# The adaLN sums of a diffusion trunk step: folding half of each accumulator into the other half in place, and summing the remaining rows with products of ones

## The chip, the core and the metric

The kernel runs on one core of a Trainium2 chip. The core has a tensor engine (TensorE, PE in the profile; its weight loads are the line PEld), a vector engine (VectorE, DVE), a scalar engine (ScalarE, ACT), GpSimd (POOL), a queue engine that starts most transfers (SyncE, SP) and sixteen DMA engines. The metric is the device time of one execution in microseconds (us); the median of three runs is used.

## The reference, cut to what matters

One step of a trunk of two layers. Each layer is feed-forward, mixer, feed-forward, and each of these three is modulated by a shift, a scale and a gate. These nine vectors come from the conditioning: silu(c) for the 256 latent tokens and silu(c_ctx) for the 128 context tokens, times a matrix of 1024 x 9216 per layer, plus a bias.

```python
def part(i):
    return mod[:, i][:, None, :]            # mod = silu(c) @ w_ada + b_ada, nine parts of 1024

h = rmsnorm(x, p['g_ff1']) * (1 + part(1)) + part(0)
x = x + 0.5 * part(2) * swiglu(h, p['w1_gate'], p['w1_up'], p['w1_down'])
h = rmsnorm(x, p['g_mix']) * (1 + part(4)) + part(3)
y, ctx_state = mixer(h)
x = x + part(5) * y
h = rmsnorm(x, p['g_ff2']) * (1 + part(7)) + part(6)
x = x + 0.5 * part(8) * swiglu(h, p['w2_gate'], p['w2_up'], p['w2_down'])
```

Everything is in float32. The kernel computes each large product as three products of rounded parts (high x high, high x low, low x high).

## The kernel before, in words

**Large products.** The state is held transposed, 1024 features on partitions in 8 tiles, 384 tokens along the row. The functions `ffn` and `mixer` load weights in chunks of 128 x 1024 on the SP queue (L234), split each chunk into a rounded part `hi` (ScalarE, L243) and a rest `lo` (VectorE, L244), and multiply: `prod3` issues three matmuls of a 128x128 weight tile with 384 columns (L248 to L250). Four buffers of `hi` and four of `lo` hold the chunks, so the vector engine is at most two pairs of chunks ahead of TensorE. The tiles `pg` and `pu` are the gate and up products, `pd` the down product; L568 multiplies silu(gate) by up into `sg`.

**The conditioning product.** For a product with only two columns (the context and the latent stream) the kernel does not use TensorE, except for the first 16 feature tiles of layer 0. It is made beside the feed-forwards as a filler. A unit is up to three tiles of 128 output features (`units`): `ada_steps` loads 128 x 8 x 384 numbers of `w_ada` into one of two `flat` buffers (L264), and then in eight steps `ada_product` (L276 for the first step, L278 for the other seven) accumulates on VectorE, for each stream s, the eight row blocks times the conditioning value of each partition into `acc[:, s, :]` (tile `adacc`, 128 partitions x 2 streams x 384, two buffers that the units use in turn). What then remains is to sum each column of `acc` over its 128 partitions. There are 43 units: 42 of three tiles and one of two.

**The sum over partitions before.** `ada_reduce` (L295) does it in two stages. In the first, two transfers on the GpSimd queue (L298, L299) copy the lower half of stream 0 and the upper half of stream 1 crosswise into the tile `adfold`, and GpSimd adds the other halves to them (L302, one addition for each stream). The tile then holds 64 partial sums of stream 0 on the upper partitions and 64 of stream 1 on the lower ones, 384 columns. In the second stage TensorE transposes its three 128x128 tiles (L308) into a PSUM tile, ScalarE sums each half row of it with an accumulating activation (L310, six per unit), and VectorE adds the bias and multiplies by the gain (`ada_finish`, L268 and L269), which gives the tile `mod`.

**What sets the order.** The class `Filler` paces the units: the loops of `ffn` call it with a fixed number of steps for each chunk. When a unit's eighth step is done its first stage is issued, and the second is kept in the list `late` with a count of six steps; `flush` counts it down with each further step and then issues the second stage, marked to be placed after the latest product step (`tc.issue_after`). The mixer calls `flush(99)` (L766), which issues all that is left. A scheduler places all instructions on the five in-order queues by the order of issue and its own costs. The places that the prediction speaks of are the TensorE queue around L308, the vector queue around L276 and L268, and the GpSimd queue around L298 to L302. A row sum of another kind also counts: `rms_sum` (L416) sums a 128x384 tile over its partitions as three matmuls of 128x128 weights with a single column of ones; and L907 and L1081, in the mixer, are matmuls that contract over only 64 partitions.

Of the kernel before, what the change touches and what calls it, by code (L numbers as in the profile page):

```python
# [9 lines left out]
F32 = mybir.dt.float32  # L10
# [3 lines left out]
AF = mybir.ActivationFunctionType  # L14
ALU = mybir.AluOpType
AX = mybir.AxisListType

P = 128
# [72 lines left out]
def trunk_kernel(ctx: ExitStack, tc: tile.TileContext, I: dict, C: dict, O: list):  # L91
    nc = tc.nc
    V, S, G, T = nc.vector, nc.scalar, nc.gpsimd, nc.tensor
# [7 lines left out]
    sm = ctx.enter_context(tc.tile_pool(name="sm", bufs=2))  # L101
# [7 lines left out]
    def small(name):  # L109
        return psm.tile([P, 512], F32, tag="sm", name=name)  # L110
# [4 lines left out]
    def cload(name, shape, src, pool=None, eng=None):  # L115
        t = (pool or const).tile(shape, F32, name=name)
        (eng or nc.gpsimd).dma_start(out=t, in_=src)
        return t
# [46 lines left out]
    ident = cload("ident", [P, P], C["ident"], eng=nc.scalar)  # L165
    cols_b0 = columns("b0", [("b_ada0", row128(I["b_ada"][0:1]), 72, nc.scalar), ("g_ff1", row128(I["g_ff1"]), 16, nc.scalar)])
    ones = const.tile([P, P], F32, name="ones")
# [90 lines left out]
    junk = const.tile([P, P], F32, name="junk")  # L258
# [7 lines left out]
    def ada_finish(l, kt, n, sums):  # L266
        mp = mod[:, l, kt:kt + n, :]
        V.tensor_tensor(out=mp, in0=sums.rearrange("p (k s) -> p k s", s=2), in1=bc(badd[:, l, kt:kt + n].unsqueeze(2), [P, n, 2]), op=ALU.add)  # L268
        V.tensor_tensor(out=mp, in0=mp, in1=bc(bmul[:, l, kt:kt + n].unsqueeze(2), [P, n, 2]), op=ALU.mult)  # L269
# [24 lines left out]

    def ada_reduce(acc, l, kt, n):  # L295
        c = n * P
        fold = sm.tile([P, 3 * P], F32, tag="adfold", bufs=1, name="adfold")
        nc.gpsimd.dma_start(out=fold[0:64, :c], in_=acc[64:128, 0, :c])  # L298
        nc.gpsimd.dma_start(out=fold[64:128, :c], in_=acc[0:64, 1, :c])  # L299
        for s in range(2):  # L300
            h = slice(64 * s, 64 * s + 64)
            G.tensor_tensor(out=fold[h, :c], in0=acc[h, s, :c], in1=fold[h, :c], op=ALU.add)  # L302

        yield False
        pm = sm.tile([P, 6], F32, tag="adasum", bufs=2, name="adasum")
        pt = small(f"ada{l}_{kt}")
        for m in range(n):
            T.transpose(pt[:, m * P:(m + 1) * P], fold[:, m * P:(m + 1) * P], ident)  # L308
        for m in range(2 * n):
            S.activation(out=junk[:, 0:64], in_=pt[:, m * 64:(m + 1) * 64], func=AF.Identity, accum_out=pm[:, m:m + 1])  # L310
        ada_finish(l, kt, n, pm[:, :2 * n])

    def ada_steps(l, kt, n, stage):

        w = stage(n)
        ada_load(w, l, kt, n)
        yield True
        acc = ada_acc()
        for k in range(KD):
            ada_product(acc, w, n, k)  # L320
            if k < KD - 1:
                yield True
        red = ada_reduce(acc, l, kt, n)
        next(red)
        yield red
# [12 lines left out]
    class Filler:  # L338
# [24 lines left out]
        def flush(self, steps):  # L363
            for t in list(self.late):
                t[0] -= steps
                if t[0] < 0:
                    self.late.remove(t)
                    with tc.issue_after(last_step[0].ins):
                        next(t[1], None)

        def begin(self):
            for _ in range(2):
# [1301 lines left out]
```

## Time and profile before

| | |
|---|---|
| median of three runs | 1611.67 us (1611.38 to 1614.06) |
| profiled execution | 1614.9 us, span of its instructions 1613.1 us |
| granted TensorE clock, mean | 0.991 of full speed |
| TensorE | 97% of the span busy |
| VectorE | 77% |
| ScalarE | 49% |
| GpSimd | 16% |

The profile is of one execution. Times are in us from the start of the span. A row of a timeline gives the start, the time covered, the engine, the line of the kernel, the operation and its tiles (output <- input), and a count when several alike follow each other. A matmul of float32 operands that isn't one of the `prod3` kind stands twice in the trace, as two passes; a transpose stands once. Matmuls overlap, so what an insertion costs is read from the starts of the matmuls around it and not from the durations.

### The profile page before, as it was taken

The numbers are of one execution on the slowest core, as the hardware profiler recorded it, in microseconds if no ns is written. First come the engines' busy times: TensorE is split into PE (matmuls) and PEld (weight loads), VectorE is DVE, ScalarE is ACT, GpSimd is POOL, SyncE is SP. The second block draws the span as 40 slices with busy tenths as digits, with TensorE's granted clock in tenths as the row PEclk, the third lists the DMA queues.
The fourth block names the chain that finished last, engine by engine and source line by source line (L and its number), as shares of the span: only waits on it lengthen the run. The fifth ranks groups of instructions, "written<-read, shape, count | busy, mean of one in ns | idle before, by whom it ended". The sixth has DMA issues, their size and how long they took to land. (4 is left out here: it accounts for less than half of the span.)

```text
span 1613.1 us, 24761 instructions
## 1 busy us (share of the span) xinstructions
PE 1561.6 (97%) x9027; PEld 1467.4 (91%) x9027; DVE 1245.8 (77%) x2485; ACT 786.8 (49%) x1838; POOL 255.4 (16%) x334
## 2 busy tenths in 40 slices
PE   7899999999999999999999999999999999999997
PEld 5789989997867999999999999999886799999997
DVE  5799997997878699996999977698787767434333
ACT  5544434548465554444546344454846656333332
POOL 2112221232040001131220212123004000000000
PEclk9999999999999999999999999999999999999999
DMA  9757758664432367867676865675344234444341
GB/s 309 247 151 232 225 185 247 208 199 120 121 75 75 109 204 232 253 179 222 212 206 192 250 195 164 213 231 158 116 111 86 66 110 126 122 126 131 118 137 46
DMA packets 233375, 270.68 MB, mean 168 GB/s; under 512 B 12392, under 2 KB 217936, under 8 KB 233253
## 3 DMA queue, kind: packets, MB, share of 16 engines
q1 hardware_dynamic: 223232, 248.67, 50.8%
q0 software_dynamic: 9744, 20.31, 5.3%
q8 instruction: 71, 1.16, 0.3%
q14 instruction: 52, 0.42, 0.1%
q10 hardware_dynamic: 276, 0.11, 0.0%
HBM read 257.10 MB, written 3.57 MB: 162 GB/s over the span
## 5 line engine op out<-in xcount | busy, mean ns | idle before, releaser
L278 DVE SCALAR_TENSOR_TENSOR adacc<-flat,sc,adacc 128x384 f32<-128x384 f32 (+1 forms) x602 | 357.2, 646 | 0.0
L302 POOL TENSOR_TENSOR adfold<-adacc,adfold 64x384 f32<-64x384 f32 (+1 forms) x86 | 118.0, 1372 | 174.7 <-DMA adfold<-adacc 172.3
L253 ACT CAST ah<-sg 128x384 fp32r<-128x384 f32 x88 | 45.1, 513 | 163.1 <-DVE sg L568 162.3
L250 PE MATMUL pd<-ah,lo_db 128*128 128x384 f32 x352 | 118.8, 338 | 1.6 <-DVE lo_db L244 1.4
L250 PE MATMUL pd<-ah,lo_da 128*128 128x384 f32 x352 | 118.7, 337 | 1.6 <-DVE lo_da L244 1.6
L249 PE MATMUL pg<-wide,hi_gb 128*128 128x384 f32 (+1 forms) x352 | 119.3, 339 | 0.2
L248 PE MATMUL pd<-ah,hi_da 128*128 128x384 f32 x352 | 119.3, 339 | 0.0
L248 PE MATMUL pg<-wide,hi_gb 128*128 128x384 f32 (+1 forms) x352 | 119.2, 339 | 0.0
L248 PE MATMUL pd<-ah,hi_db 128*128 128x384 f32 x352 | 118.9, 338 | 0.0
L250 PE MATMUL pg<-wide,lo_gb 128*128 128x384 f32 (+1 forms) x352 | 118.5, 337 | 0.0
L249 PE MATMUL pu<-wide,hi_ub 128*128 128x384 f32 (+1 forms) x352 | 118.4, 336 | 0.0
L249 PE MATMUL pd<-al,hi_db 128*128 128x384 f32 x352 | 118.4, 336 | 0.0
L249 PE MATMUL pd<-al,hi_da 128*128 128x384 f32 x352 | 118.4, 336 | 0.0
L248 PE MATMUL pu<-wide,hi_ub 128*128 128x384 f32 (+1 forms) x352 | 118.2, 337 | 0.0
L250 PE MATMUL pu<-wide,lo_ub 128*128 128x384 f32 (+1 forms) x352 | 117.8, 337 | 0.0
L248 PE MATMUL pu<-wide,hi_ua 128*128 128x384 f32 (+1 forms) x328 | 111.3, 340 | 4.2 <-DVE sg L568 4.2
L250 PE MATMUL pg<-wide,lo_ga 128*128 128x384 f32 (+1 forms) x328 | 112.0, 343 | 1.9 <-DVE lo_ga L244 1.9
L248 PE MATMUL pg<-wide,hi_ga 128*128 128x384 f32 (+1 forms) x328 | 113.5, 346 | 0.0
L249 PE MATMUL pg<-wide,hi_ga 128*128 128x384 f32 (+1 forms) x328 | 112.0, 342 | 0.0
L298 POOL DMA_DIRECT2D adfold<-adacc x43 | 23.9, 556 | 550.5 <-DVE adacc L278 352.0
L249 PE MATMUL pu<-wide,hi_ua 128*128 128x384 f32 (+1 forms) x328 | 110.9, 338 | 0.0
L250 PE MATMUL pu<-wide,lo_ua 128*128 128x384 f32 (+1 forms) x328 | 110.6, 338 | 0.0
(504 smaller groups left out, 4290.9 us busy)
## 6 DMA issues: line engine op xcount, KB each, us to landing
flat<-in_w_ada_dram SPq DMA_DIRECT2D x42, 1536.0 KB, 8.1
st_gb<-in_w_gate_dram SPq DMA_DIRECT2D x44, 512.0 KB, 3.8
st_ub<-in_w_up_dram SPq DMA_DIRECT2D x44, 512.0 KB, 4.5
st_ga<-in_w_gate_dram SPq DMA_DIRECT2D x41, 512.0 KB, 3.9
st_ua<-in_w_up_dram SPq DMA_DIRECT2D x41, 512.0 KB, 4.9
st_da<-in_w_down_dram SPq DMA_DIRECT2D x40, 512.0 KB, 4.8
st_db<-in_w_down_dram SPq DMA_DIRECT2D x40, 512.0 KB, 3.5
wst<-in_w_ada_dram SPq DMA_DIRECT2D x8, 1024.0 KB, 12.6
```

The lines of the kernel that those rows point to most:

```text
L248: T.matmul(out, lhsT=lh, rhs=rh, start=start, stop=False)
L249: T.matmul(out, lhsT=lh, rhs=rl, start=False, stop=False)
L250: T.matmul(out, lhsT=ll, rhs=rh, start=False, stop=stop)
L253: S.copy(hi, src)
L278: last_step[0] = V.scalar_tensor_tensor(out=acc[:, s, :n * P], in0=w[:, k, :], scalar=sc[:, k, s:s + 1], in1=acc[:, s, :n * P], op0=ALU.mu ...
L298: nc.gpsimd.dma_start(out=fold[0:64, :c], in_=acc[64:128, 0, :c])
L302: G.tensor_tensor(out=fold[h, :c], in0=acc[h, s, :c], in1=fold[h, :c], op=ALU.add)
```

## The change

The copies crosswise and the GpSimd additions become two transfers that add into the accumulator itself: the lower half of stream 0 is added to its upper half, and the upper half of stream 1 to its lower half. The tile `adfold` and its additions go. In the second stage the transposes and the six accumulating activations go; instead, for each stream, up to three matmuls take 64 partitions x 128 columns of the accumulator as the stationary operand and a 64x1 column of ones as the moving one, and give the 128 sums of a tile directly as a column of PSUM; ScalarE copies three such columns at a time. The generator now yields its own delays (2 steps between the matmuls and `ada_finish`), and `flush` goes on with a unit as long as its delay is over.

```diff
     def ada_reduce(acc, l, kt, n):
         c = n * P
-        fold = sm.tile([P, 3 * P], F32, tag="adfold", bufs=1, name="adfold")
-        nc.gpsimd.dma_start(out=fold[0:64, :c], in_=acc[64:128, 0, :c])
-        nc.gpsimd.dma_start(out=fold[64:128, :c], in_=acc[0:64, 1, :c])
+        nc.gpsimd.dma_start(out=acc[0:64, 0, :c], in_=acc[64:128, 0, :c], accum_op=ALU.add)
+        nc.gpsimd.dma_start(out=acc[64:128, 1, :c], in_=acc[0:64, 1, :c], accum_op=ALU.add)
+
+        yield 2
+        pm = sm.tile([P, 6], F32, tag="adasum", bufs=2, name="adasum")
         for s in range(2):
             h = slice(64 * s, 64 * s + 64)
-            G.tensor_tensor(out=fold[h, :c], in0=acc[h, s, :c], in1=fold[h, :c], op=ALU.add)
-
-        yield False
-        pm = sm.tile([P, 6], F32, tag="adasum", bufs=2, name="adasum")
-        pt = small(f"ada{l}_{kt}")
-        for m in range(n):
-            T.transpose(pt[:, m * P:(m + 1) * P], fold[:, m * P:(m + 1) * P], ident)
-        for m in range(2 * n):
-            S.activation(out=junk[:, 0:64], in_=pt[:, m * 64:(m + 1) * 64], func=AF.Identity, accum_out=pm[:, m:m + 1])
+            pt = small(f"ada{l}_{kt}")
+            for m in range(n):
+                T.matmul(pt[:, m:m + 1], lhsT=acc[h, s, m * P:(m + 1) * P], rhs=ones[h, 0:1], start=True, stop=True)
+            S.copy(pm[:, s:2 * n:2], pt[:, :n])
+        yield 2
         ada_finish(l, kt, n, pm[:, :2 * n])
...
         def flush(self, steps):
             for t in list(self.late):
                 t[0] -= steps
-                if t[0] < 0:
-                    self.late.remove(t)
+                while t in self.late and t[0] < 0:
                     with tc.issue_after(last_step[0].ins):
-                        next(t[1], None)
+                        more = next(t[1], None)
+                    if more is None:
+                        self.late.remove(t)
+                    else:
+                        t[0] += more
```

On TensorE, at the unit whose sums are the tile `ada0_31` (layer 0, feature tiles 31 to 33), between the products of two weight chunks, the order before is:

```order
L249 MATMUL pu1_1875<-wide3_229,hi_ua07_0_1884 128x384
L250 MATMUL pu1_1875<-wide2_228,lo_ua07_0_1885 128x384
L308 MATMUL ada0_31_1988<-ident_92,adfold_1907 128x128 [waits PE_49,Pool_49]
L308 MATMUL ada0_31_1988<-ident_92,adfold_1907 128x128 x2
L248 MATMUL pg0_1872<-wide2_228,hi_ga07_4_1969 128x384
L249 MATMUL pg0_1872<-wide3_229,hi_ga07_4_1969 128x384
```

and in the changed kernel (L306 is its line of the products with ones):

```order
L249 MATMUL pu1_1860<-wide3_229,hi_ua07_0_1869 128x384
L250 MATMUL pu1_1860<-wide2_228,lo_ua07_0_1870 128x384
L306 MATMUL ada0_31_1970<-ones_97,adacc_1728 128x1 [waits DMASW4_49,PE_49]
L306 MATMUL ada0_31_1970<-ones_97,adacc_1728 128x1 x2
L306 MATMUL ada0_31_1975<-ones_97,adacc_1728 128x1 [waits DMASW5_49,PE_49]
L306 MATMUL ada0_31_1975<-ones_97,adacc_1728 128x1 x2
L248 MATMUL pg0_1857<-wide2_228,hi_ga07_4_1951 128x384
L249 MATMUL pg0_1857<-wide3_229,hi_ga07_4_1951 128x384
```

The place is the same; six products stand where three transposes stood, and they wait for the two transfers where the transposes waited for GpSimd.

On VectorE, where the accumulator of a new unit is first written (L276) while the sums of an earlier one are finished (L268, L269), the order before is:

```order
L568 TENSOR_TENSOR sg_1488<-sg_1488,pu1_1314 128x384 [waits PE_49,Activation_49]
L244 TENSOR_TENSOR lo_ua05_4_1603<-st_ua05_4_1600,hi_ua05_4_1602 128x1024 [waits DMAHW3_49,Activation_49]
L254 TENSOR_TENSOR al9_670<-sg_1488,ah9_669 128x384 [waits Activation_49]
L276 TENSOR_SCALAR adacc_1608<-flat1_1417,sc_99 128x384 [waits DMASW5_49,DMAHW4_49,DMASW4_49,Pool_49]
L276 TENSOR_SCALAR adacc_1608<-flat1_1417,sc_99 128x384
L278 SCALAR_TENSOR_TENSOR adacc_1608<-flat1_1417,sc_99,adacc_1608 128x384 [waits DVE_49] x2
L268 TENSOR_TENSOR mod_104<-adasum_1524,badd_101 128x6 [waits Activation_49]
```

and in the changed kernel:

```order
L254 TENSOR_TENSOR al9_670<-sg_1479,ah9_669 128x384 [waits Activation_49]
L244 TENSOR_TENSOR lo_ua05_4_1591<-st_ua05_4_1588,hi_ua05_4_1590 128x1024 [waits DMAHW3_49]
L268 TENSOR_TENSOR mod_104<-adasum_1515,badd_101 128x6 [waits Activation_49]
L276 TENSOR_SCALAR adacc_1596<-flat1_1408,sc_99 128x384 [waits DMASW5_49,DMAHW4_49,DMASW4_49,PE_49]
L269 TENSOR_TENSOR mod_104<-mod_104,bmul_102 128x6 [waits DVE_49]
L276 TENSOR_SCALAR adacc_1596<-flat1_1408,sc_99 128x384
L278 SCALAR_TENSOR_TENSOR adacc_1596<-flat1_1408,sc_99,adacc_1596 128x384 [waits DVE_49] x10
```

The first write of a reused accumulator waited for GpSimd's additions and now waits for TensorE, which reads the accumulator itself.

## Rows read from the trace of the kernel before

**Rows 1.** The page: busy time of each engine, share of the span, instructions

```profile
PE 1561.6 (97%) x9027; PEld 1467.4 (91%) x9027; DVE 1245.8 (77%) x2485; ACT 786.8 (49%) x1838; POOL 255.4 (16%) x334
```

**Rows 2.** Busy time by stretch: start:end, length, each engine, clock, DMA

```profile
200.00:300.00 100.00, 96.58 (x561) 95.67 (x561) 89.51 (x144) 41.47 (x108) 23.92 (x24) 1.00 0.71 221
...
1400.00:1500.00 100.00, 100.00 (x579) 100.00 (x578) 42.19 (x49) 36.11 (x48) 0.00 (x0) 1.00 0.44 127
```

**Rows 3.** Timeline of TensorE around the transposes of a unit

```profile
1010.76 0.34 PE L250 MATMUL pu<-wide,lo_ua 128*128 128x384 f32 x1
1010.94 0.49 PE L308 MATMUL ada<-ident,adfold 128*128 128x128 f32 x3
...
1011.44 0.34 PE L249 MATMUL pg<-wide,hi_ga 128*128 128x384 f32 x1
```

**Rows 4.** Line 308: all its transposes, duration min/median/max in ns

```profile
L308 PE MATMUL ada<-ident,adfold x128: 271/272/330, 114.5 to 1144.6; 128*128 128x128 f32 x128
```

**Rows 5.** Timeline of TensorE around a row sum over 128 partitions

```profile
563.61 0.34 PE L250 MATMUL pu<-wide,lo_ub 128*128 128x386 f32 x1
563.78 0.73 PE L416 MATMUL stb<-ones,accb 128*128 128x1 f32 x6
...
564.63 0.34 PE L249 MATMUL pg<-wide,hi_gb 128*128 128x386 f32 x1
```

**Rows 6.** Timeline of TensorE: four products over 64 partitions, in two blocks

```profile
395.86 0.71 PE L907 MATMUL pP<-qk 64*128 64x128 f32 x8
396.51 0.44 PE L912 MATMUL pk<-ident,qk 128*128 128x128 f32 x2
```

**Rows 7.** Timeline of the weight loads of these products

```profile
395.80 0.58 PEld L907 LDWEIGHTS pP<-qk 64*128 64x128 f32 x8
```

**Rows 8.** Line 907: all its weight loads, duration min/median/max in ns

```profile
L907 PEld LDWEIGHTS pP<-qk x16: 183/188/220, 395.8 to 1162.5; 64*128 64x128 f32 x16
```

**Rows 9.** Timeline of TensorE: out of 64-wide products, and into products over 64 partitions

```profile
1234.24 0.45 PE L248 MATMUL pdu<-wide,hi_du 128*128 128x384 f32 x1
1234.52 0.34 PE L249 MATMUL pdu<-wide,hi_du 128*128 128x384 f32 x1
...
1235.22 0.34 PE L250 MATMUL pdu<-wide,lo_du 128*128 128x384 f32 x1
1235.49 0.92 PE L1081 MATMUL s<-qT 64*128 64x384 f32 x4
```

**Rows 10.** What TensorE waited for: us in total, times, longest

```profile
PE pu L248 <- DVE sg L568: 4.2, 4, 2.1
...
PE pd L250 <- DVE lo_da L244: 1.6, 3, 1.2
...
PE pd L250 <- DVE lo_db L244: 1.4, 2, 1.2
```

**Rows 11.** Waits of VectorE: us in total, times, longest

```profile
DVE adacc L276 <- POOL adfold L302: 12.2, 6, 6.6
...
DVE mod L268 <- ACT junk L310: 9.0, 10, 3.3
```

**Rows 12.** Timeline of GpSimd: the two additions of a unit

```profile
221.84 2.63 POOL L302 TENSOR_TENSOR adfold<-adacc,adfold 64x384 f32<-64x384 f32 x2 [5.72 <-DMA adfold<-adacc]
```

**Rows 13.** Timeline of VectorE at the same time

```profile
223.52 0.97 DVE L269 TENSOR_TENSOR mod<-mod,bmul 128x6 f32<-128x6 f32 x1
```

**Rows 14.** Line 269: all its instructions, duration min/median/max in ns

```profile
L269 DVE TENSOR_TENSOR mod<-mod,bmul x51: 149/163/1018, 21.1 to 1160.0; 128x6 f32<-128x6 f32 x42, 128x4 f32<-128x4 f32 x9
```

**Rows 15.** Timeline of GpSimd: a unit's second copy issued, its last addition

```profile
187.42 0.52 POOL L299 DMA_DIRECT2D adfold<-adacc  x1
...
192.63 1.90 POOL L302 TENSOR_TENSOR adfold<-adacc,adfold 64x384 f32<-64x384 f32 x1 [0.53 <-DMA adfold<-adacc]
```

**Rows 16.** Timeline of TensorE: the transposes of the same unit

```profile
194.58 0.55 PE L308 MATMUL ada<-ident,adfold 128*128 128x128 f32 x3
```

**Rows 17.** The copies into `adfold`: time from issue to landing

```profile
DMA to landing us min/median/max: 2.0/4.4/8.0
```

## The prediction

> **What bounds the kernel now.** I read the page first, for the share of each engine. TensorE is busy for 97% of the span, VectorE for 77%, ScalarE for 49%, GpSimd for 16% [rows 1]. Then the busy time by stretch. In the last feed-forward, where no conditioning unit runs, TensorE is busy without a gap and does 579 matmuls in 100 us, one each 0.173 us [rows 2]; that is the pace of the large products. In the first feed-forward, where units run, it is busy for 96.6 of 100 us. So nearly everything that is put into TensorE's queue between the large products lengthens the run by what it takes, and an engine beside it counts only where TensorE waits for it. The third view is TensorE's waits by what ended them: those that VectorE ends in the feed-forwards beside the units come to 4.2 + 1.6 + 1.4 = 7.2 us [rows 10]. This is all that a faster VectorE can give back there.
>
> **What goes from TensorE.** The 128 transposes [rows 4], three for each of 42 units and two for the last. Their price is read from the starts around them. From the last L250 before them to the second matmul after them the trace has 1011.44 - 1010.76 = 0.68 us [rows 3]; without them these would be two steps of the pace, 0.346 us. So a unit's transposes cost 0.334 us, 14.3 us for 128.
>
> **What comes to TensorE.** For a unit of three tiles six products of 64 partitions x 128 columns with one column of ones, at the place of the transposes. They are float32, so each is two passes with a weight load each: twelve passes. The trace has no such product with one column. Its nearest rows bound the price:
> - From above, the row sum over 128 partitions, also one column. Its six passes stretch 0.346 us to 564.63 - 563.61 = 1.02 us [rows 5]: 0.67 us, 0.112 us for a pass. A column costs almost nothing, so this is the pace of weight loads that follow each other.
> - Nearer, four products over 64 partitions: first two on the lower 64 partitions, then two on the upper, also float32, also 128 columns of weights. Eight passes take 396.51 - 395.86 = 0.65 us to the start of the next matmul, 0.081 us each [rows 6]. They have 128 moving columns and are still cheaper than 0.112, and the reason is in their loads: eight loads of 0.188 us each [rows 8] are 1.50 us, and they fit into 0.58 us [rows 7]. The loads of the two halves overlap.
> - From below, half of the nearer price, 0.04 us, if moving one column instead of 128 saves as much as the loads allow.
>
> I take 0.081 us, as the new products come in the same two blocks, lower half and then upper. To this comes the change between the full array and the half one. Going into products over 64 partitions, the step is 1235.49 - 1235.22 = 0.27 us and so 0.10 above the pace; coming back from narrower products, 1234.52 - 1234.24 = 0.28 us, 0.11 above it [rows 9]. Together 0.20 us for a unit.
>
> A unit then costs 12 x 0.081 + 0.20 = 1.17 us where it cost 0.334: +0.84 us. The unit of two tiles costs 8 x 0.081 + 0.20 = 0.85 instead of 0.22: +0.63. Over the run 42 x 0.84 + 0.63 = **+36 us** on TensorE. By the bounds: with 0.112, 1.54 us a unit and +52 us; with 0.04, 0.68 us a unit and +15 us.
>
> The Trainium skill speaks against the middle value: its page TensorE: Matmul & The Clock Gate (LDWEIGHTS) says that the time of a weight load goes by its columns and not by its rows, so that half a height saves nothing; twelve loads at its 107 ns are by estimate 1.28 us, and the sum near the upper bound. Its page TensorEngine Tiling (Array Packing) (Key Properties) says that different tiles of the array can load weights and multiply in parallel, and by that the sum is nearer to the middle. The rows fit both: a load over 64 partitions is not short in itself, and two halves do overlap. What the pages leave open is how far the overlap goes when one half's loads all come before the other's.
>
> **What the other engines get.** The order of the changed kernel shows the products where the transposes stood, so on TensorE nothing else moves in the feed-forwards. In the mixers some products of the first part change places; they stay beside the same waits, and I count them as nothing, with 3 us to either side.
>
> VectorE gains three things. Its first write of a reused accumulator no longer waits for GpSimd's additions (12.2 us in all), and `ada_finish` comes two steps later and no longer right behind ScalarE's sums (9.0 us in all) [rows 11]. And its small instructions no longer run beside GpSimd's additions: an L269 that took 0.97 us [rows 13], 0.163 us in the median [rows 14], stands in the middle of a pair of additions [rows 12]. TensorE can get from this no more than its 7.2 us [rows 10]; I take 5, as the slower TensorE itself also uses up such waits. **-5 us.**
>
> VectorE also gets a wait: the first write of a reused accumulator now waits for TensorE's products. Behind it in VectorE's queue stand the splits of the next weight chunks, and TensorE waits for these. What hides it: in the order shown the write comes behind the split of a chunk that needs the buffer which TensorE leaves last before the very same products, so TensorE is about there when VectorE arrives. Where it is not, the wait is at most half a chunk's products, 12 x 0.173 = 2.1 us, while TensorE has at least one chunk of products ready. I count it at nothing; were all 41 reuses to cost TensorE 0.2 us, it would be 8 us.
>
> On ScalarE two small copies take the place of six accumulating activations; at 49% it is on no path here. On GpSimd the additions go, and so do its waits for landing copies, so the transfers are issued no later than before. On SyncE seven of the `w_ada` loads stand a few places later, behind weight loads; each still has another unit's time before it is read. Nothing for these.
>
> The transfers that add read the destination as well. They have to land before TensorE arrives. In the tightest unit that I found the second copy was issued at 187.42, the last addition was over at 194.53 [rows 15], and the transposes began at 194.58 [rows 16]: 7.2 us for a transfer alone, as the additions fall away. Copies landed after 2.0 to 8.0 us, 4.4 in the median [rows 17]. I take it that adding transfers land in under 7 us. Nothing for these either.
>
> **Sum.** +36 - 5 = +31 us. Made against the profiled execution, of 1614.9 us with a span of 1613.1, that is 1646 us. This execution was 3.2 us above the median of the runs, 1611.67, so I predict **1643 us**.
>
> **Rivals.**
> - *Loads one behind the other.* The two halves do not overlap because the upper half's first product waits for its own transfer, or because only neighbours overlap. For: the waits at both blocks, and the 0.112 us of rows 5. Against: the products of rows 6 have the same two blocks. Then +52 - 5 = +47: 1659 us.
> - *Late transfers.* TensorE arrives at the products before the added data, and the large products queue behind. For: the gap of 7.2 us is below the longest landing of a copy, 8.0. Against: GpSimd's additions took 2 us or more of the former path. It decides from a landing of 7.2 us on. At three times the copies' median, 13.2 us, a unit as tight as this waits 6 us; with one unit in six like it, 7 x 6 = 42 us more: 1685 us.
> - *VectorE decides, faster.* TensorE's new passes disappear beside the large products, so that a unit costs only the change to the half array and back, 0.20 us, and TensorE regains all its waits for VectorE. The place is the stretch from 200 to 300 us, where TensorE is at 96.6%. Then 42.7 x (0.20 - 0.334) = -5.7 and -7.2 make -13 us: 1599 us. It decides when a unit's products cost less than 0.334 + 7.2 / 42.7 = 0.50 us. For: rows 12 to 14. Against: six passes of the row sum cost 0.67 us in the midst of the same large products; they did not disappear.
> - *Cheap passes.* The price of 0.04 us: +15 - 5 = +10: 1622 us.
>
> **Chances and range.** Forecast 0.58, with its own range 1631 to 1653; loads one behind the other 0.18; cheap passes 0.11; late transfers 0.07; VectorE decides 0.06. The range from 1621 to 1666 holds the forecast and the loads wholly and about half of the cheap passes, and leaves out the late transfers and the faster case. A measurement of this kernel can tell about 0.2% from no change, 3.2 us. Faster by more than that needs the third rival or the cheap passes at their lowest with all waits regained: 0.05. Within it, the border between these: 0.04. Slower: 0.91.
>
> **What would show it.** In the changed profile the products with ones should be 512 passes (42 x 12 + 8), and around a block of twelve the steps should stretch by about 1.17 us: 1.5 means that the loads do not overlap, 0.7 that passes are cheap. TensorE's waits by VectorE's `sg` and `lo` lines should shrink below 3 us, those for the adding transfers should be absent, and VectorE's first accumulator write should wait for TensorE by little. The forecast is wrong if a unit's block costs under 0.5 us, or if TensorE is seen waiting for transfers at its products.

## The result: 21 us slower, in the forecast's range

The changed kernel takes 1634.02 us (median of 4 runs, 1633.58 to 1636.59), the kernel before 1612.87 us beside it (4 runs, 1611.38 to 1614.35). The ratio is 1.0149 with a 95% interval of 1.013 to 1.0169; the medians lie 21 us apart. Forecast were 1643 us, 31 above 1612, with a range from 1621 to 1666. The direction and the price on TensorE are right; the sum is 10 us too high, because more of that price was hidden than forecast.

The profiled execution of the changed kernel took 1633.79 us with a span of 1632.0, 18.9 us longer than the one before. Its page, busy time of each engine; this answers to [rows 1]:

```profile
PE 1592.5 (98%) x9411; PEld 1495.4 (92%) x9411; DVE 1203.8 (74%) x2485; ACT 727.7 (45%) x1412; POOL 162.6 (10%) x248
```

TensorE runs 384 more instructions (512 passes for 128 transposes) and is busy 31 us longer; every other engine got lighter. The same stretches as in [rows 2], columns as there:

```profile
200.00:300.00 100.00, 100.00 (x604) 98.68 (x603) 84.23 (x151) 35.60 (x58) 9.98 (x13) 1.00 0.73 220
...
1400.00:1500.00 100.00, 100.00 (x579) 100.00 (x578) 42.07 (x48) 36.03 (x48) 0.00 (x0) 1.00 0.44 127
```

The 3.4 us in which TensorE stood idle in the first feed-forward are gone. So two things happened in one stretch: its queue got longer, and its gaps closed. First the length. TensorE's timeline around a unit, to be held against [rows 3]:

```profile
1060.27 0.34 PE L250 MATMUL pd<-ah,lo_da 128*128 128x384 f32 x1
1060.54 1.08 PE L306 MATMUL ada<-ones,adacc 64*128 64x1 f32 x12
1061.54 0.44 PE L248 MATMUL pd<-ah,hi_da 128*128 128x384 f32 x1
1061.82 0.34 PE L249 MATMUL pd<-al,hi_da 128*128 128x384 f32 x1
```

From the last L250 to the second matmul behind the block are 1.55 us, less two steps of the pace (0.346) 1.20 us; the transposes cost 0.334. In it are the step into the half array (0.27 us), the twelve passes (1.00 us to the next start, 0.083 each) and the step back (0.28 us).

Then the gaps. I added up over all of TensorE's starts by how much a step exceeds the pace of 0.173 us, the units' blocks apart. All blocks together cost 15.0 us before and 51.7 us after, **+36.6 us**; all other excess was 44.9 us before and 27.6 us after, **-17.3 us**. The two make the +19 between the profiles (19.3, the rest lies behind the last matmul). Of the 17.3, 14.7 are in the two feed-forwards beside units (23.4 before, 8.7 after; 96 to 360 and 504 to 1141 us of the trace before), 3.2 in the mixers; elsewhere the change lost 0.6 us more.

What one such gap looks like, in TensorE's timeline of the kernel before:

```profile
205.19 0.34 PE L250 MATMUL pg<-wide,lo_ga 128*128 128x384 f32 x1
207.68 0.44 PE L248 MATMUL pu<-wide,hi_ua 128*128 128x384 f32 x1 [2.15 <-DVE sg L568]
207.97 0.33 PE L249 MATMUL pu<-wide,hi_ua 128*128 128x384 f32 x1
```

The list of waits counts 2.15 us. By the starts TensorE lost 2.43: 2.78 us stand where two steps of 0.173 would. The drawn end of a matmul lies a step beyond the next one's start, and the first step after a pause is 0.11 longer.

VectorE, which had to make `sg` (L568), did not pause from 195 to 208 us. Its timeline there, in part, and GpSimd's:

```profile
203.24 1.37 DVE L278 SCALAR_TENSOR_TENSOR adacc<-flat,sc,adacc 128x384 f32<-128x384 f32 x1
204.53 0.97 DVE L268 TENSOR_TENSOR mod<-adasum,badd 128x6 f32<-128x6 f32 x1
...
207.09 0.54 DVE L568 TENSOR_TENSOR sg<-sg,pu 128x384 f32<-128x384 f32 x1
```

```profile
202.79 2.69 POOL L302 TENSOR_TENSOR adfold<-adacc,adfold 64x384 f32<-64x384 f32 x2 [4.82 <-DMA adfold<-adacc]
```

Beside GpSimd's two additions an L278 took 1.37 us (median of all: 0.61) and an L268 0.97 (median 0.17): 1.6 us of the 2.43. TensorE's three next largest losses to VectorE beside units, at 226, 344 and 829 us (1.5 us each by the starts), also come behind instructions that ran long beside additions, with VectorE busy without a pause from these on.

VectorE's waits in the changed kernel, which answer to [rows 11] (both kinds there are gone):

```profile
DVE adacc L276 <- PE ada L306: 17.5, 22, 2.1
```

And the adding transfers (engine, count, size, median us to landing), against the copies' 4.4 us in [rows 17]:

```profile
adacc<-adacc POOLq DMA_DIRECT2D x84, 96.0 KB, 6.7
```

### The profile page after: what moved, and what is told of

Its sections match the earlier page's. It is cut to its first block, busy times and chain, and to the rows that moved or that the text cites. A ratio compares the mean times of both kernels' runs of the same rounds, so it can differ in the third digit from the quotient of the medians.

```text
span 1632.0 us, 25079 instructions
## 1 busy us (share of the span) xinstructions
PE 1592.5 (98%) x9411; PEld 1495.4 (92%) x9411; DVE 1203.8 (74%) x2485; ACT 727.7 (45%) x1412; POOL 162.6 (10%) x248
## 3 DMA queue, kind: packets, MB, share of 16 engines
q8 instruction: 74, 1.21, 0.3%
## 4 chain that ended last, share of the span: by engine, by line
PE 88%; DVE 4%; issue 3%; ACT 3%; DMA 1%; POOL 1%; ACTq 0%; POOLq 0%
PE pg L248 8%; PE pd L248 8%; PE pg L249 7%; PE pg L250 7%; PE pd L250 7%; PE pd L249 7%; PE pu L249 7%; PE pu L250 7%; PE pu L248 7%; PE ada L306 3%; PE pwo L248 1%; PE pwo L249 1%; PE pwo L250 1%; PE pa L772 1%; PE pa L773 1%
## 5 line engine op out<-in xcount | busy, mean ns | idle before, releaser
L278 DVE SCALAR_TENSOR_TENSOR adacc<-flat,sc,adacc 128x384 f32<-128x384 f32 (+1 forms) x602 | 333.1, 608 | 0.0
L250 PE MATMUL pg<-wide,lo_gb 128*128 128x384 f32 (+1 forms) x352 | 118.3, 336 | 0.0
L250 PE MATMUL pd<-ah,lo_da 128*128 128x384 f32 x352 | 118.3, 336 | 0.0
L250 PE MATMUL pd<-ah,lo_db 128*128 128x384 f32 x352 | 118.3, 336 | 0.0
L249 PE MATMUL pd<-al,hi_da 128*128 128x384 f32 x352 | 118.2, 336 | 0.0
L250 PE MATMUL pu<-wide,lo_ub 128*128 128x384 f32 (+1 forms) x352 | 117.7, 336 | 0.0
L297 POOL DMA_DIRECT2D adacc<-adacc x43 | 35.4, 824 | 788.7 <-issue 338.4
L250 PE MATMUL pg<-wide,lo_ga 128*128 128x384 f32 (+1 forms) x328 | 110.5, 338 | 1.9 <-DVE lo_ga L244 1.9
L250 PE MATMUL pu<-wide,lo_ua 128*128 128x384 f32 (+1 forms) x328 | 110.3, 337 | 0.0
L244 DVE TENSOR_TENSOR lo_gb<-st_gb,hi_gb 128x1024 fp32r<-128x1024 f32 x44 | 53.8, 1224 | 66.4 <-ACT hi_gb L243 66.4
L244 DVE TENSOR_TENSOR lo_db<-st_db,hi_db 128x1024 fp32r<-128x1024 f32 (+1 forms) x48 | 54.4, 1133 | 62.7 <-ACT hi_db L243 62.7
## 6 DMA issues: line engine op xcount, KB each, us to landing
wst<-in_w_ada_dram SPq DMA_DIRECT2D x8, 1024.0 KB, 12.6
```

The source lines that it names most:

```text
L244: V.tensor_tensor(out=lo[:, :n], in0=st[:, :n], in1=hi[:, :n].bitcast(F32), op=ALU.subtract)]
L249: T.matmul(out, lhsT=lh, rhs=rl, start=False, stop=False)
L250: T.matmul(out, lhsT=ll, rhs=rh, start=False, stop=stop)
L278: last_step[0] = V.scalar_tensor_tensor(out=acc[:, s, :n * P], in0=w[:, k, :], scalar=sc[:, k, s:s + 1], in1=acc[:, s, :n * P], op0=ALU.mu ...
L297: nc.gpsimd.dma_start(out=acc[0:64, 0, :c], in_=acc[64:128, 0, :c], accum_op=ALU.add)
```

## The experiments

All times are medians with runs of the kernel before on the same chip beside them; its medians there were 1612.59 us for the first four experiments, 1611.18 for the next four and 1610.45 for the last two. The table gathers what the sections use: what the units cost TensorE over the kernel before (summed over starts, as above), how much longer the kernel took, the difference of the two (swallowed), and TensorE's other excess in the feed-forwards beside units (23.4 us before).

| kernel | units, us | time, us | ratio, 95% interval | swallowed, us | other excess, us |
|---|---|---|---|---|---|
| the change | +36.6 | +21.2 | 1.0149 (1.013 to 1.0169) | 15.4 | 8.7 |
| additions gone | -0.1 | -7.3 | 0.9945 (0.9925 to 0.9965) | 7.2 | 9.2 |
| products on fold | +36.6 | +22.0 | 1.0126 (1.0106 to 1.0146) | 14.6 | 12.6 |
| longer units | +32.0 | +18.3 | 1.011 (1.0091 to 1.0129) | 13.7 | 12.1 |
| halves in turn | +26.5 | +8.9 | 1.0056 (1.0036 to 1.0076) | 17.6 | 7.4 |
| light sums | -0.1 | -4.1 | 0.9978 (0.9962 to 0.9995) | 4.0 | 22.8 |
| longer still | +71.7 | +54.6 | 1.0335 (1.0316 to 1.0353) | 17.1 | 10.1 |
| full rows | +42.6 | +30.3 | 1.0181 (1.0161 to 1.0201) | 12.3 | 7.4 |
| masked ones | +13.9 | -2.2 | 0.9989 (0.9976 to 1.0002) | 16.1 | 7.3 |
| both | +32.0 | +22.5 | 1.0139 (1.0123 to 1.0155) | 9.5 | 7.8 |
| sums on VectorE | +0.4 | -5.8 | 0.996 (0.9945 to 0.9976) | 6.2 | 12.4 |

The interval of a ratio is 2 to 3 us to either side, and the profiles are of one execution each; so the column of what was swallowed can't tell 14 us from 16.

The first three take the change apart: where did the 15 us come from?

### Additions gone

```
 # VectorE multiplies by scw: sc with the two streams exchanged on partitions 64 to 127
-        nc.gpsimd.dma_start(out=fold[0:64, :c], in_=acc[64:128, 0, :c])
-        nc.gpsimd.dma_start(out=fold[64:128, :c], in_=acc[0:64, 1, :c])
-        for s in range(2): ... G.tensor_tensor(... op=ALU.add)
+        nc.gpsimd.dma_start(out=acc[0:64, 0, :c], in_=acc[64:128, 1, :c], accum_op=ALU.add)
+        nc.gpsimd.dma_start(out=acc[64:128, 0, :c], in_=acc[0:64, 1, :c], accum_op=ALU.add)
...
-            T.transpose(pt[:, m * P:(m + 1) * P], fold[:, m * P:(m + 1) * P], ident)
+            T.transpose(pt[:, m * P:(m + 1) * P], acc[:, 0, m * P:(m + 1) * P], ident)
```

> Half of the change: GpSimd's additions go and transfers that add come, but the three transposes and ScalarE's six sums stay. (VectorE multiplies by a copy of the conditioning in which the two streams are exchanged on the upper 64 partitions, so that two adding transfers fold both streams into one 128-partition tile.) TensorE's order is that of the kernel before. In the trace of the change TensorE paid 36.6 us more for the units, but lost 17.3 us less elsewhere, where I had forecast 5. Theory A, the additions held VectorE up and that is where TensorE's other losses came from: they go here too, without the 36.6 us, so 1613 - 13 to 17 = 1596 to 1600 us. Theory B, the losses came from ScalarE's six sums and the modulation that waits for them: nothing changes, 1611 to 1615 us. Theory C, the losses vanished because a longer TensorE gives the other engines time: 1611 to 1615 us as well.

Measured: 1605.32 us against 1612.59, 7.3 us faster: between the theories. In the feed-forwards it behaves as theory A says, the excess falls from 23.4 to 9.2 us, 14 us less. The profile gives half of it back elsewhere: 2.5 us more in the mixers and 2.7 us more ahead of the first unit, partly in stretches of a granted clock of 0.50. The amount of these differs between executions of one kernel: the mean granted clock of the kernel before lay between 0.986 and 0.993 in the runs beside this one. Why the mixers lose is not settled.

### Products on the fold buffer

```
 # copies into fold and GpSimd's additions as before
-            T.transpose(pt[:, m * P:(m + 1) * P], fold[:, m * P:(m + 1) * P], ident)
-        for m in range(2 * n): S.activation(...)
+        for s in range(2):
+            h = slice(64 * s, 64 * s + 64)
+            pt = small(f"ada{l}_{kt}")
+            for m in range(n):
+                T.matmul(pt[:, m:m + 1], lhsT=fold[h, m * P:(m + 1) * P], rhs=ones[h, 0:1], start=True, stop=True)
+            S.copy(pm[:, s:2 * n:2], pt[:, :n])
```

> The other half of the change: the copies into the fold buffer and GpSimd's additions stay, the transposes and ScalarE's six sums become twelve half-row passes and two small copies. TensorE's units cost 36.6 us more, as in the change. Theory A (the additions are the cause of TensorE's other losses): the losses stay, 1613 + 37 = 1648 to 1652 us. Theory B (ScalarE's sums are): they go, 1632 to 1636 us, as the change. Theory C (a longer TensorE hides them): 1632 to 1637 us.

Measured: 1634.55 us, the time of the whole change. Theory A falls as the sole cause: with the additions in place the same 15 us are swallowed. Beside the products, adding transfers in place of additions are worth nothing that shows (22.0 against 21.2 us over before).

### Longer units

```
 # behind the three transposes and six sums of the kernel before
+        for s in range(2):
+            h = slice(64 * s, 64 * s + 64)
+            pd = small(f"pad{l}_{kt}_{s}")
+            for m in range(2):
+                T.matmul(pd[:, m:m + 1], lhsT=fold[h, m * P:(m + 1) * P], rhs=ones[h, 0:1], start=True, stop=True)
```

> The kernel before with eight half-row passes more in each unit, behind the three transposes, whose results nothing reads. Additions and sums stay as they were; only TensorE's queue gets longer. Eight passes and the change of mode were 0.76 us in the unit of two tiles of the changed kernel, 43 x 0.76 = 32 us. Theories A and B: 1613 + 32 = 1643 to 1647 us, nothing is hidden. Theory C (a longer TensorE gives VectorE time and so hides its waits): some 10 to 14 us less, 1630 to 1635 us.

Measured: 1630.93 us, 18.3 over before, though by the starts the units cost exactly the expected 32.0 us more. Theory C holds, and B is not needed: neither additions nor sums were touched, and 13.7 us vanish. The busy time of the engines (TensorE, its loads, VectorE, ScalarE, GpSimd) in a stretch with units, in the kernel before:

```profile
126.00:260.00 134.00, 130.58 (x753) 127.89 (x753) 126.25 (x203) 60.11 (x161) 35.98 (x37) 1.00 0.66 203
```

in the kernel without additions:

```profile
126.00:260.00 134.00, 134.00 (x777) 132.21 (x776) 117.00 (x207) 62.48 (x161) 17.14 (x21) 1.00 0.73 219
```

and with longer units:

```profile
126.00:260.00 134.00, 133.94 (x799) 130.55 (x798) 121.90 (x196) 57.86 (x156) 35.75 (x36) 1.00 0.68 209
```

In the kernel before VectorE was busy for 126 of 134 us, 94%, so it had little room to make up for a delay. Its waits did not get less with longer units; it still stood 12.3 us for the additions, as before (12.2, [rows 11]):

```profile
DVE adacc L276 <- POOL adfold L302: 12.3, 6, 5.1
```

These waits are not what TensorE had lost to: in the kernel before the six lie between 675 and 1076 us, and TensorE's list of waits has one place behind them, at 962 us (0.66 us by the starts). What vanished are losses behind instructions that ran long. They still run long (the longest L278 took 1.43 us here, 1.40 before), but from 126 to 260 us of the trace before TensorE lost 4.9 us, and at the same products here 1.5. TensorE just no longer arrives before VectorE is through.

### Halves in turn

```
-        for s in range(2):
-            for m in range(n):
+        pts = [small(f"ada{l}_{kt}_{s}") for s in range(2)]
+        for m in range(n):
+            for s in range(2):
+                h = slice(64 * s, 64 * s + 64)
                 T.matmul(pts[s][:, m:m + 1], lhsT=acc[h, s, m * P:(m + 1) * P], rhs=ones[h, 0:1], ...)
```

> The change with the six products in another order: lower half, upper half, lower half and so on, in place of three of the lower and then three of the upper. In the trace of the change the starts within one half are 0.112 us apart, and the upper half starts 0.25 us behind the lower and runs beside it. Theory D, each half is a queue of its own at 0.112 us a pass, and the upper half's late start is part of the price: the block shrinks by some 0.19 us, 43 x 0.19 = 8 us, 1624 to 1628 us. Theory E, twelve passes come at 0.083 us each however they are ordered, as one stream: 1632 to 1636 us. If only loads of different halves overlap (the forecast's reason for the middle price), alternating makes it cheaper as well, 0.04 to 0.06 us a pass, 1615 to 1625 us.

Measured: 1621.44 us, 12.6 less than the change and beyond theory D's 8. By the starts the blocks cost 41.5 us in place of 51.7, 10.2 less (0.97 a unit for 1.21), and theory D names the reason. (The range of the last variant holds the time too; its 0.04 to 0.06 us for a pass does not hold the 0.064 that follow below.) TensorE's timeline around a block:

```profile
1048.90 0.34 PE L250 MATMUL pd<-ah,lo_da 128*128 128x384 f32 x1
1049.16 0.83 PE L306 MATMUL ada<-ones,adacc 64*128 64x1 f32 x12
1049.93 0.45 PE L248 MATMUL pd<-ah,hi_da 128*128 128x384 f32 x1
1050.21 0.34 PE L249 MATMUL pd<-al,hi_da 128*128 128x384 f32 x1
```

The twelve passes take 0.77 us in place of 1.00. The passes that run in each quarter of a microsecond show how (a pass counts in every stretch that it touches). The change, lower half first:

```profile
1060.50:1060.75 0.25, 0.21 (x2) 1.00 0.92 108
1060.75:1061.00 0.25, 0.25 (x6) 1.00 0.43 62
1061.00:1061.25 0.25, 0.25 (x8) 1.00 0.23 86
```

and in turn:

```profile
1049.15:1049.40 0.25, 0.24 (x4) 1.00 0.23 74
1049.40:1049.65 0.25, 0.25 (x10) 1.00 0.49 141
1049.65:1049.90 0.25, 0.25 (x8) 1.00 0.46 129
```

In the change the lower half works alone at first, two passes 0.13 us apart, and the upper one starts 0.25 us behind it; in turn both start within 0.01 us, and the passes come in pairs, 0.11 us apart.

### Full rows

```
-        (the two adding transfers)
-                T.matmul(pt[:, m:m + 1], lhsT=acc[h, s, m * P:(m + 1) * P], rhs=ones[h, 0:1], ...)
+                T.matmul(pt[:, m:m + 1], lhsT=acc[:, s, m * P:(m + 1) * P], rhs=ones[:, 0:1], ...)
```

> The change without its adding transfers: six products with ones over all 128 partitions, on the accumulator itself, at the same places; still twelve passes, in one row of the array. Theory D, a row of the array takes a pass each 0.112 us, and the halves' price came from running beside each other: 12 x 0.112 + 0.09 for coming back = 1.43 us a unit instead of 1.21, 43 x 0.22 = 9.5 us over the change, 1641 to 1645 us. Theory E, 0.083 us for a pass of one column in any form, and no change of mode: 12 x 0.083 + 0.09 = 1.09 us, 1627 to 1631 us. If the adding transfers cost anything beside their landing, both come out lower by that.

Measured: 1641.45 us; theory D's. The block in TensorE's timeline:

```profile
1065.37 0.34 PE L250 MATMUL pd<-ah,lo_da 128*128 128x384 f32 x1
1065.55 1.39 PE L301 MATMUL ada<-ones,adacc 128*128 128x1 f32 x12
1066.80 0.42 PE L248 MATMUL pd<-ah,hi_da 128*128 128x384 f32 x1
1067.06 0.34 PE L249 MATMUL pd<-al,hi_da 128*128 128x384 f32 x1
```

A unit costs 1.69 - 0.346 = 1.34 us, 0.112 for each of twelve passes, with no change of mode, where the expectation had 1.43. So with its halves one behind the other the change saved 0.14 us a unit against this, and in turn 0.37.

### Light sums

```
-  V.scalar_tensor_tensor(out=acc[:, s, :n * P], in0=w[:, k, :], ..., in1=acc[:, s, :n * P], ...)
+  V.scalar_tensor_tensor(out=acc[:, s, :n * 64], in0=w[:, k, :n * 64], ..., in1=acc[:, s, :n * 64], ...)
```

> The kernel before with VectorE's accumulating products of the units over half their columns (so half of each sum is left out); additions, transposes and ScalarE's sums stay, and TensorE's order changes only ahead of 120 us. It asks where TensorE's losses beside the units come from. Theory C, VectorE is late because its work for a unit takes longer than TensorE's products beside it: with some 150 us less of that work the losses go without any change on TensorE, 1612.6 - 14 = 1596 to 1600 us. Theory F, only the collisions with GpSimd's additions make VectorE late, which were worth 7 us when the additions went alone: less accumulating takes away little of these, 1605 to 1612 us.

Measured: 1607.04 us, 4 us faster: in theory F's range, and theory C's simple form (VectorE has too much to do) misses by 8. The profiled execution took 1614.34 us, 7 above this median, so its trace shows where time goes and not the 4 us. In it VectorE's work fell by 137 us, and yet TensorE's other excess beside units stayed, 22.8 us, though at other places. Where the trace before lost 12.4 us (126 to 360 and 751 to 1141 us), this one lost 3.8, as theory C says. But 7 us are new, in the stretch that runs from 617 to 751 us in the trace before, where that lost nothing; and from 96 to 126 us 9.1 are lost, where it was 8.4. VectorE's waits over the run, columns as in [rows 11]:

```profile
DVE adacc L276 <- POOL adfold L302: 90.8, 23, 8.6
```

A lighter VectorE is sooner at the next unit's accumulator, which GpSimd has not yet read, and stands there 23 times instead of 6; behind it in its queue are the splits and gatings that TensorE needs. Twice, after 8.3 and 8.6 us, `sg` came right behind such a wait, and TensorE lost 1.6 and 2.5 us. So both make VectorE late, its load and its queue stopped by GpSimd's late additions; in this execution the second took back what less of the first had given.

### Longer still

```
 # against the longer units
-            for m in range(2):
-                T.matmul(pd[:, m:m + 1], lhsT=fold[h, m * P:(m + 1) * P], ...)
+            for m in range(4):
+                T.matmul(pd[:, m:m + 1], lhsT=fold[h, m % 2 * P:(m % 2 + 1) * P], ...)
```

> The kernel before with sixteen half-row passes more in a unit in place of the eight that cost TensorE 32 us and the run 18. Eight more of these are by the starts in the trace 4 x 0.112 = 0.45 us for each unit, 19 us. Theory C in the form that a fixed stock of some 14 us of waits is used up: all 19 are seen, 1630.9 + 19 = 1648 to 1652 us. Theory G, a fixed share of whatever is added hides (14 of 32): 1612.6 + 51 x 0.57 = 1640 to 1643 us.

Measured: 1665.73 us, far above both expectations, because the price was wrong. TensorE's timeline around the sixteen passes:

```profile
1033.29 0.49 PE L308 MATMUL ada<-ident,adfold 128*128 128x128 f32 x3
1033.71 1.52 PE L315 MATMUL pad<-ones,adfold 64*128 64x1 f32 x16
1035.16 0.45 PE L248 MATMUL pg<-wide,hi_ga 128*128 128x384 f32 x1
```

and around the eight of the experiment before:

```profile
1021.79 0.49 PE L308 MATMUL ada<-ident,adfold 128*128 128x128 f32 x3
1022.21 0.62 PE L315 MATMUL pad<-ones,adfold 64*128 64x1 f32 x8
1022.75 0.45 PE L248 MATMUL pg<-wide,hi_ga 128*128 128x384 f32 x1
```

Eight passes take 0.54 us, sixteen 1.45. By the starts the second half begins 0.01 us behind the fourth-last pass of the first; with four of each that is at once, with eight of each 0.47 us late. With the price that the starts show (+71.7 us) the run speaks for the fixed stock: 17.1 us are swallowed, where a share of 14 in 32 would be 31.

### Masked ones

```
 # scw and the two adding transfers as in the kernel without additions; hm: 128 x 2, a one per half
-            T.transpose(...)
-        for m in range(2 * n): S.activation(...)
+            T.matmul(pt[:, 2 * m:2 * m + 2], lhsT=acc[:, 0, m * P:(m + 1) * P], rhs=hm, start=True, stop=True)
+        S.copy(pm[:, :2 * n], pt[:, :2 * n])
```

> GpSimd's additions and ScalarE's six sums both gone, and TensorE's products over the full height: the streams are exchanged on the upper partitions as in the experiment without additions, two adding transfers fold them into one tile of 128 partitions, and three products with a two-column mask of ones give both sums at once: six passes, one copy. By the row sum's six passes a unit costs 0.67 us instead of 0.34 for the transposes, 14 us more. Theory C, what is hidden is a stock of 14 to 17 us: 1612.6 + 14 - 14 = 1610 to 1614 us. If only the 7 us of the missing additions come back: 1618 to 1621 us.

Measured: 1608.98 us against 1611.18, no difference that counts (the interval reaches 1.0002). The price is as expected, 13.9 us, and 16.1 are swallowed: the stock again.

### Both, and the sums on VectorE

The kernel without additions, once with the eight passes of the longer units (on `acc[h, 0]`), once with ScalarE's six sums made by one instruction:

```
-        for m in range(2 * n): S.activation(...)
+        V.tensor_reduce(out=pm[:, :2 * n], in_=pt[:, :n * P].rearrange("p (k t) -> p k t", t=64), axis=AX.X, op=ALU.add)
```

> Two of the experiments put together: the additions gone (adding transfers, transposes and ScalarE's sums, 7 us faster alone) and eight half-row passes more in each unit (32 us of TensorE, of which 18 were seen and 14 hidden). Theory C', one stock of waits, which either edit uses up: 1612.6 + 32 - 14 to 17 = 1627 to 1631 us, as with the longer units alone. Theory H, two gains of different origin, which add up: 1612.6 + 32 - 14 - 7 = 1623 to 1625 us.

> The kernel without additions, and ScalarE's six sums made by one VectorE instruction over the transposes' result, which goes ahead of the unit's modulation on the same engine. TensorE's units cost 15 us as in the kernel before. If a stock of 14 us or more is to be had without any lengthening of TensorE, and ScalarE's chain held part of it: 1597 to 1602 us. If what the other engines can give back alone is the 7 us of the missing additions: 1603 to 1607 us.

Measured: both together 1632.92 us against 1610.45, 22.5 over before. Theory H (they add up; 10 to 12 over) falls. Theory C' (14 to 18 over) is nearer and still 4 us short: the two together swallow 9.5 us, less than the longer units alone. In its feed-forwards nothing is left to swallow (7.8 us of excess, which agrees with one stock), but outside them it loses almost 4 us more than the kernel before, where the kernel without additions lost 6 more; why is open. Sums on VectorE: 1604.69 us, 5.8 faster, no more than without additions alone. No gain from ScalarE's chain shows; as VectorE took on 23.6 us of work for the sums, a small one may be hidden. The kernel without additions beats both kernels, at 0.9945 of before, with this last one beside it.

## Why the prediction was right, and which term was off

- **Transposes, 14.3 us.** Right: the blocks sum to 15.0 us, some in mixers.
- **Products, 1.17 us a unit, +36 us.** Right in size: 1.20 us, +36.6. The steps came as read from the nearest rows: into the half array 0.10 over the pace, back 0.11 [rows 9]. A pass came at 0.083 us where 0.081 was taken [rows 6], and that was luck, as there is no price per pass: eight cost 0.54 us, twelve 1.00, sixteen 1.45, or 0.77 for twelve in turn. A half takes a pass each 0.112 us, the price of rows 5, and the halves run beside each other once the second has started. In rows 6, with four passes a half, both start 0.01 us apart, and their eight passes of 128 columns took 0.65 us where eight of one column take 0.54; in the change the upper half starts 0.25 us late. Slower passes there and a late half here came out alike. The length of the loads, from which the prediction read the overlap, doesn't show it: loads over the full height last 0.191 us in the mean (full rows) and follow each other at 0.112 as well.
- The rival *loads one behind the other* is refuted: in the change the upper half's passes start between the lower's, and twelve take 1.00 us. In the full rows they do come one behind the other, at 1.34 us a unit and 1641 us. The two rules of the Trainium skill that were set against each other both hold. The Trainium skill's page TensorE: Matmul & The Clock Gate (LDWEIGHTS) says that a load's time goes by columns and not by rows; the trace agrees, 0.188 us for a load over 64 rows and 0.191 over 128, and 0.112 us for a pass at either height. The Trainium skill's page TensorEngine Tiling (Array Packing), Key Properties, says that tiles of the array load and multiply in parallel; the halves in turn agree, with pairs of passes 0.01 us apart.
- **VectorE's relief, -5 us, at most 7.2.** This step failed: "TensorE can get from this no more than its 7.2 us". It got 15 (17 by the profiles). Two errors are in it. The ceiling was too low: the listed 7.2 us are some 10 by the starts, and the first units' stretch (96 to 126 us) was left out but for 0.4 us of them, where before lost 8.4 us and after 3.1 (light sums 9.1, the other traces 3.1 to 4.9). Two stretches at a granted clock of 0.50 (1.2 GHz) are in it, from 103.5 and from 120.6 us on, each shortly behind pauses of TensorE (0.56 and 0.51 us; 1.7 us), and a large product takes 0.32 us in them for 0.173. The whole stretch in the kernel before:

```profile
96.00:126.00 30.00, 27.69 (x128) 24.07 (x127) 25.57 (x47) 10.52 (x29) 6.83 (x10) 0.89 0.73 210
```

and in the changed one, with 163 matmuls for 128 (twelve of them a unit's passes with ones, where before has three transposes) and no clock lost:

```profile
96.00:126.00 30.00, 29.44 (x163) 26.29 (x162) 28.28 (x53) 11.07 (x23) 5.40 (x7) 1.00 0.77 230
```

  And the credit was given to one cause where each of two is enough. I asked what a faster VectorE gives back (without additions: 14 us in the feed-forwards, 7 in the time); but a longer TensorE gives the same back by itself (13.7 us, longer units), and the products alone as much as the whole change (14.6). The prediction named the slower TensorE only as a reason to take less. In the sum "+36 on TensorE" and "-5 by VectorE" were taken as independent terms, while the first draws on the stock that the second speaks of.
- **VectorE's new wait, 0.** Right: 17.5 us at 22 reuses, the longest 2.1, exactly the bound, and TensorE is busy without a gap beside it.
- **Adding transfers, 0.** Right in effect, no wait of TensorE for them is in the trace; the landing was taken too short ("under 7 us": median 6.7, longest 9.3). What saved it is that the room was longer than read: 8.7 us from issue to products in the tightest unit (issued at 118.2 us), whose transfer landed after 8.2, 0.5 us ahead of them; in every other unit it landed 4 us ahead or more.
- **Mixers, 0 with 3 to either side.** The profiles have 3.2 us less. Kernels without additions but in the old order had 1.6 to 2.5 us more. Half-clock stretches are in both; not settled.
- The sum with the measured terms: 36.6 - 15.4 = 21.2 us, by construction; by the profiles alone 36.6 - 17.3 = 19.3.

## What to carry to other kernels

When the bounding engine also waits here and there for others, what lengthens its own queue first uses up these waits: price an edit as its length less the stock of waits around it, and read that stock from the starts against the pace, not from the list of waits. Here it was 9.5 to 17.6 us in the eight kernels whose TensorE units got 14 to 72 us longer. Such a stock is spent once, whichever edit spends it. And products like these, three or more on each half of the array, should be issued in turn, not half by half.

## What the hardware showed that I had not expected

- Float32 passes of one column on one half follow each other at 0.112 us, as on the full array, and the halves overlap. Issued half by half, the second half starts 0.01 us behind the fourth-last pass of the first, in every unit whose records are complete: with two products (four passes) each at once, with three 0.25 us late, with four 0.47 us late. Issued in turn there is no delay.
- VectorE's accumulating instruction was faster without GpSimd's additions. The row of the page before (count, busy us, mean ns):

```profile
L278 DVE SCALAR_TENSOR_TENSOR adacc<-flat,sc,adacc 128x384 f32<-128x384 f32 (+1 forms) x602 | 357.2, 646 | 0.0
```

and after:

```profile
L278 DVE SCALAR_TENSOR_TENSOR adacc<-flat,sc,adacc 128x384 f32<-128x384 f32 (+1 forms) x602 | 333.1, 608 | 0.0
```

  With longer units and the additions kept it was 650 ns, without additions and with the old sums 613: the additions cost it 20 to 24 us over the run. The Trainium skill, SBUF — State Buffer (SBUF: two separate sides), says that VectorE instructions with two SBUF inputs and GpSimd instructions that read SBUF share a pair of ports, which one of them holds for a whole instruction. The rows agree: the longest L278 took 1.40 us before and 0.62 after.
- A transfer that adds landed after 6.7 us in the median and kept GpSimd 0.82 and 1.11 us at its issue, where a copy took 4.4 and 0.53.
